# Two plain fp32 channel tiles at the start, two shift rows on TensorE, and a shorter norm in a two-layer hybrid decoder

## The chip, the cores and the metric

The kernel runs on one core of one Trainium2 chip. The metric is the device time of one execution in microseconds (us), lower is better. A core has five engines with a queue each that is worked in order: PE (TensorE, matrix products; its weight loads are listed as PEld), DVE (VectorE), ACT (ScalarE), POOL (GpSimd) and SP (SyncE, which here only issues transfers). On this kernel a difference of less than about 0.3% (3 us) cannot be told from no change.

## The reference, cut to what matters

Two layers, sequence of 256 tokens, width 1024, fp32. `rms_norm` without its gain is folded with the modulation, and `h` feeds one wide input projection and later the FFN:

```python
mod = c_act @ w_ada[l] + b_ada[l]
sh1, sc1, gt1, sh2, sc2, gt2 = jnp.split(mod, 6, axis=-1)
h = modulate(rms_norm(x, norm_mix[l]), sh1, sc1)     # h * (1 + scale) + shift
p = h @ w_in[l]
# p -> dilated attention, RWKV-7 scan, chunked spatial gating, three branch gates -> merged
x = x + gt1[:, None, :] * (merged @ w_out[l])
h = modulate(rms_norm(x, norm_ffn[l]), sh2, sc2)
x = x + gt2[:, None, :] * conv_gated_ffn(h, ...)
# after the last layer: rms_norm(x, norm_final)
```

## The kernel before

Activations lie transposed: a channel tile is 128 channels by 256 tokens, and a product over the width of 1024 adds eight of them (`k` = 0 to 7). To be near fp32 in accuracy at the speed of fp32r, every operand is split in a high part (rounded to fp32r, a CAST) and a low part (the difference, a subtraction on DVE), and one product becomes three fp32r matmuls, `mm3`: high weight by high activation, high weight by low activation, low weight by high activation. The activations' parts are `hhi` and `hlo`; the weights' are `whi` and `wlo` in steady state, with `raw` and `m` as landing buffers.

The conditioning vector is turned into rows of `mod` by `ada_col`: for each block of 128 outputs either one pass of DVE over a 128x1024 block (SCALAR_TENSOR_TENSOR with an accumulator, `w` times `crow`) or eight matmuls on PE, in fp32, with one moving column (`eng == "PE"`). `ADA_ENG` chooses; before, DVE does all.

The start is special. Before anything of layer 0 can be multiplied, `x` is loaded, its squares are summed (`rstd`: squares on ACT, sums on DVE and PE, a power on POOL, a transposing matmul that spreads the result, and a copy to `rS`), and the scale and shift of channel tile `k` must be known. `SEQ` sets the order of the 28 transfers of 512 KB in that stage: for each `k` two blocks A (scale and shift of tile k) and one or two half blocks W of the weights, so that product `k` of the first six chunks (`START` = 6, `gemm_side`, twelve weight cells of 128x128 for each `k`) can run when its A and W are there. Written out: A0 A0' W0 W1 A1 A1' W2 A2 A2' W3 W4 A3 A3' W5 and so on to W11, the accent marking the shift's block. `setup` issues all this, splits the W blocks into buffers borrowed from later stages (`dests`), and calls `norm_h`, which makes `hhi` and `hlo` of each tile.

At the other three norms the work goes through `ahead`: two chunks of the next product (`AHEAD` = 2) are multiplied with `x * A` before the norm's `rS` is known (`gemm_ahead`, 96 matmuls, operands `yrh`, `yrl`, `ygh`, `ygl`), `finish` scales the result later (tile `gate`), and `norm_h` makes the rest's operands meanwhile. In layer 1, the first of these chunks gives `zx`, whose tanh feeds the products with `lora`.

None of this is issued in the order of the code. Every operation is recorded in a `Plan` with a cost and its dependencies; `flush` runs a list scheduler a hundred times with shaken priorities, keeps the best of its own estimates and then emits each engine's queue. `P.boost` raises priorities. An operation recorded by `copy` or `ts` may be given to ACT or DVE (`either`); `act` goes to ACT alone, unless it is a Copy or Identity whose scale is a column. So any edit of costs or operations reorders all queues of the program.

Of the kernel before, what the change touches and what calls it, by code (L numbers as in the profile page):

```python
# [12 lines left out]
F32 = mybir.dt.float32  # L13
F32R = mybir.dt.float32r
# [6 lines left out]
S = 256  # L21
# [40 lines left out]
]  # L62
AHEAD = 2
START = 6
SEQ = []
for _k in range(8):
    SEQ += [("A", _k, 0), ("A", _k, 1)]
# [3 lines left out]
HOLD, SHORT, WAIT, URGENT = ("DVE",), 0.5, 0.15, 10.0  # L71
BOOST = {'ahead': 30, 'norm': 100, 'rstd': 3}
MAIN = False
ADA_ENG = [['DVE'] * 8, ['DVE'] * 8]
ADA_AT = [7, 9, 11, 11, 18, 18, 22, 22, 22, 24, 24, 30] + [39 + i * 31 // 28 for i in range(28)]
ADA = []
for _l in range(L):
# [325 lines left out]
def decoder(ctx: ExitStack, tc: tile.TileContext, xT, cst_d, vec_d, wada, stream, small, lnrow, bsrow, out):  # L403
# [10 lines left out]
    def slot(tag, shape, dt=F32):  # L414

        t = pers.tile(list(shape), dt, name=f"{tag}_{len(slots.setdefault(tag, []))}", tag=tag, bufs=1)
        n = t.tensor.name
        known.add(n)
        if slots[tag]:
            last = slots[tag][-1]  # L420
            P.born[n] = {h[1] for h in P.hist.get(last, ())} | P.born.get(last, set())
        slots[tag].append(n)
        return t
# [61 lines left out]
    def mul(o, a, b):  # L485
        tt(o, a, b, OP.mult)
# [4 lines left out]
    def sub(o, a, b):  # L491
        tt(o, a, b, OP.subtract)

    def ts(o, a, s1, s2, op0, op1=None):
        if s2 is None:
            op1 = None
        ins = [a] + [x for x in (s1, s2) if x is not None and not isinstance(x, (int, float))]

        def emit():
            if op1 is None:  # L500
                nc.vector.tensor_scalar(o, a, s1, None, op0=op0)
            else:
                nc.vector.tensor_scalar(o, a, s1, s2, op0=op0, op1=op1)  # L503

        alts = [("DVE", 0.01 + 0.06 * len(ins) + _n(a) / (960 if _psum(o, a) else 1920), emit)]
        if op0 == OP.mult and op1 in (None, OP.add) and not isinstance(s1, (int, float)) and not isinstance(s2, (int, float)):
            k = {} if s2 is None else {"bias": s2}
            alts.append(("ACT", _act(a) + 0.093 * (1 + len(k)), lambda: nc.scalar.activation(
                o, a, AF.Copy if s2 is None else AF.Identity, scale=s1, **k)))
        P.either(alts, [o], ins)  # L510
# [45 lines left out]
    raws = [raws0, raws0]  # L556
    whis = [new(pers, (128, 1024), f"whi{i}", F32R) for i in range(4)]
    wlos = [new(pers, (128, 1024), f"wlo{i}", F32R) for i in range(4)]
    bdw = [slot(f"bd{i}", (128, 2048), F32R) for i in range(3)]
    rsy = [new(pers, (128, 3, 16), f"rs{i}") for i in range(3)]  # L560
    banks = {"mm": [new(psum, (128, 512), f"bkm{i}") for i in range(3)],
             "rk": [new(psum, (128, 512), f"bkr{i}") for i in range(3)],
# [7 lines left out]
    def ring(key, lst):  # L570
        i = count.get(key, 0)
        count[key] = i + 1
        return lst[i % len(lst)]
# [78 lines left out]
    def mm3(ps, wh, wl, xh, xl, first, last):  # L652
        return [(ps, wh, xh, first, False), (ps, wh, xl, False, False), (ps, wl, xh, False, last)]
# [4 lines left out]
    def hk(k):  # L658
        return hhi[:, k, :], hlo[:, k, :]
# [41 lines left out]
    def gemm_side(m):  # L701
        pss = [bank("ff") for _ in range(min(m, 6))] + banks["at"][0:max(m - 6, 0)]
        for k in range(KT):
            for c, ps in enumerate(pss):
                g = []
                for n in range(2):
                    g += [x + (1,) for x in mm3(ps[:, n * 256:(n + 1) * 256], *cells[(k * m + c) * 2 + n], *hk(k),
                                                k == 0 and n == 0, k == KT - 1 and n == 1)]
                pe(g, MAIN)
        return pss  # L710

# [43 lines left out]
        pe([(pr[:, t * 128:(t + 1) * 128], y[:, t:t + 1].to_broadcast([128, 128]), ident) for t in range(2)])  # L755
        acopy(rS, pr[:, 0:S])

    def norm_h(l, which, tmp):
        A = amod[:, l, which * 8:which * 8 + 8]
        B = mod[:, l, which * 24:which * 24 + 8]  # L760
        for k in range(KT):
            v = ring("nv", tmp)
            mul(v, x[:, k, :], rS)
            ts(v, v, A[:, k:k + 1], B[:, k:k + 1], OP.mult, OP.add)
            acopy(hhi[:, k, :], v)
            sub(hlo[:, k, :], v, hhi[:, k, :].bitcast(F32))

# [445 lines left out]
    def setup(W):  # L1215
        P.boost = 4000.0
        turn = dma(vec, vec_d)
        for j in range(4):
            turn = dma(x[:, 2 * j:2 * j + 2, :], xT[:, 2 * j:2 * j + 2, :], seq=turn)
        tc = acol[:, 0:8]  # L1220
        act(tc, ccol, AF.Tanh, scale=0.5)
        ts(tc, tc, 1.0, 0.5, OP.add, OP.mult)
        mul(ccol, tc, ccol)
        for n in range(2):
            ps = bank("mm")
            pe([(ps[:, k * 128:(k + 1) * 128], ccol[:, 4 * n + k:4 * n + k + 1].to_broadcast([128, 128]), ident)
                for k in range(4)])
            acopy(crow[:, n * 512:(n + 1) * 512], ps)
        for l in range(L):
            ts(dv[:, l, 0:14], vv(l, "mu", 0, 14), -1.0, 1.0, OP.mult, OP.add)  # L1230
            ts(dv[:, l, 14:22], vv(l, "w0", 0, 8), 0.5, None, OP.mult)
            ts(dv[:, l, 22:26], vv(l, "ka", 0, 4), -1.0, 1.0, OP.mult, OP.add)
            ts(dv[:, l, 26:34], vv(l, "bada", 8, 8), 1.0, None, OP.add)
            ts(dv[:, l, 34:42], vv(l, "bada", 32, 8), 1.0, None, OP.add)
        rstd(W["sq"])
        bufs = raws0 + [W[f"m{i}"] for i in range(4)] + ([W[n] for n in ("VK", "PB", "BK")] if START < 7 else [W["BK"], lora])
        last = []
        for t, (a, i, n) in enumerate(SEQ):
            P.boost = 3000.0 - 10 * t
            w = ring("first", bufs)  # L1240
            d = turn = dma(w, (stream if a == "W" else wada)[i][:, n * 1024:(n + 1) * 1024], seq=turn)
            P.boost = 0.0
            if a == "A":
                last.append(d)
                ada_col(*ADA[i][n], w, ADA_ENG[n][i])
                continue
            to = dests.pop(0)
            k = 1024 // len(to)
            for m, (hi, lo) in enumerate(to):
                src = w[:, m * k:(m + 1) * k]  # L1250
                acopy(hi, src)
                sub(lo, src, hi.bitcast(F32))
                cells.extend([(hi[:, o:o + 128], lo[:, o:o + 128]) for o in range(0, k, 128)])
        pos["load"] = START
        norm_h(0, 0, halves)
        return last

    W = {}
# [24 lines left out]
    def cut(hi, lo):  # L1283
        return [(hi[:, i:i + 1024], lo[:, i:i + 1024]) for i in range(0, hi.shape[1] - 1023, 1024)]
# [1 line left out]
    short = [slot(n, (128, 512), F32R) for n in ("kkn", "tt", "s20", "s21", "sig", "aa", "cs", "gt", "zk", "zr", "zv", "zx")]  # L1286
    dests += [[(a, b)] for a, b in [(whis[0], wlos[0]), (whis[1], wlos[1])]
              + [(y[0].rearrange("p a b -> p (a b)")[:, 0:1024], y[1].rearrange("p a b -> p (a b)"))
                 for y in (yrw, ygw)] + cut(bdw[0], bdw[1]) + cut(bdw[2][:, 0:1024], bdw[2][:, 1024:2048])]
    dests += [[(short[i], short[i + 1]), (short[i + 2], short[i + 3])] for i in (0, 4, 8)]  # L1290
    count["whi"] = count["wlo"] = 2
    if START > 5:
# [2 lines left out]
    if START > 6:  # L1295
        g = [slot(f"gate{i}", (128, 512), F32R) for i in range(4)]
        dests += [[(g[0], g[1]), (g[2], g[3])], [(slot("PB", (128, 1024), F32R), slot("VK", (128, 1024), F32R))]]
    del dests[2 * START:]

    head = None  # L1300
    for l in range(L):
# [267 lines left out]
```

## Time and profile before

| what | value |
|---|---|
| median of 3 runs | 1022.81 us (1021.56 to 1024.1) |
| the profiled execution, own time | 1023.31 us |
| its span, first to last instruction | 1021.5 us |
| PE busy | 975.9 us, 96% |
| DVE busy | 906.6 us, 89% |
| ACT busy | 530.2 us, 52% |
| matmul records | 7674 |
| mean granted TensorE clock | 0.987 |
| HBM read | 212.12 MB |

A product in plain fp32 appears in the profile as two records, an fp32r one as a single record. A row of the timeline gives the start in us, the time in us, the engine, the line, the operation, output and inputs, the shape, a count, and in brackets the idle time ahead of it with what ended it. A row that merges several instructions gives the time from the first start to the last end. Times of a busy PE overlap, so the spacing of starts, not the time of one, tells its rate.

### The profile page before, as it was taken

To read this page: it belongs to the slowest core of one execution; us is meant where nothing else is said; L and a number is where in the kernel's file an instruction comes from. 1 tells how busy PE (TensorE), PEld (TensorE's weight loads), DVE (VectorE), ACT (ScalarE), POOL (GpSimd) and SP (SyncE) were. 2 spreads that over 40 slices of the span, in tenths; PEclk is the share of its full clock that TensorE was granted. 3 is DMA by queue.
4 is the path that set the end of the run, shared out by engine and by line. 5 is a ranking of instruction groups with operands and counts; after the bars stand their busy time and mean duration, and the time that the engine had idled before them with its cause. 6 is when DMAs were issued, how large, how long until landed. Compare 5 with 4: busy or idle time off the path is not lost. (4 is left out here: it accounts for less than half of the span.)

```text
span 1021.5 us, 19783 instructions
## 1 busy us (share of the span) xinstructions
PE 975.9 (96%) x7674; PEld 931.3 (91%) x7674; DVE 906.6 (89%) x1913; ACT 530.2 (52%) x909; POOL 37.4 (4%) x27
## 2 busy tenths in 40 slices
PE   2999999899999999999999999999999999999996
PEld 2988989799999999998889899998999999999886
DVE  6998999999979999999999999799867789878763
ACT  4473575675544744444447465656733555343341
POOL 0020000000000000000010110100000000000000
PEclk9999999899999999999997999999999999999998
DMA  9888575566777768789894644364435646555541
GB/s 343 345 287 266 189 234 175 174 216 206 244 261 271 231 220 300 260 285 337 320 324 132 226 151 149 124 191 146 140 119 166 213 141 221 180 184 179 188 140 42
DMA packets 70126, 217.60 MB, mean 213 GB/s; under 512 B 15120, under 2 KB 17168, under 8 KB 69520
## 3 DMA queue, kind: packets, MB, share of 16 engines
q1 hardware_dynamic: 70032, 216.34, 63.3%
q8 instruction: 60, 0.98, 0.4%
q14 instruction: 34, 0.28, 0.1%
HBM read 212.12 MB, written 4.19 MB: 212 GB/s over the span
## 5 line engine op out<-in xcount | busy, mean ns | idle before, releaser
L479 ACT CAST whi<-raw 128x1024 fp32r<-128x1024 f32 x203 | 212.0, 1048 | 229.3 <-PE bkm L455 121.5
L455 PE MATMUL bkm<-hhi,whi 128*128 128x256 f32 x1104 | 321.5, 291 | 6.8 <-ACT hhi L479 5.5
L483 DVE TENSOR_TENSOR wlo<-raw,whi 128x1024 fp32r<-128x1024 f32 (+1 forms) x293 | 292.8, 1008 | 38.8 <-ACT whi L479 37.5
L455 PE MATMUL bkm<-hlo,whi 128*128 128x256 f32 x1104 | 314.3, 285 | 5.6 <-DVE hlo L483 3.9
L455 PE MATMUL bkm<-hhi,wlo 128*128 128x256 f32 x1104 | 313.9, 284 | 0.6 <-DVE wlo L483 0.6
L455 PEld LDWEIGHTS bkm<-hhi,whi 128*128 128x128 f32 x1104 | 212.9, 193 | 13.2 <-ACT hhi L479 5.9
L455 PEld LDWEIGHTS bkm<-hlo,whi 128*128 128x128 f32 x1104 | 213.0, 193 | 7.0 <-DVE hlo L483 4.5
L455 PEld LDWEIGHTS bkm<-hhi,wlo 128*128 128x128 f32 x1104 | 212.9, 193 | 1.2 <-DVE wlo L483 1.0
L455 PE MATMUL bkr<-hhi,wlo 128*128 128x256 f32 x368 | 104.2, 283 | 0.6 <-DVE wlo L483 0.6
L455 PE MATMUL bkr<-hhi,whi 128*128 128x256 f32 x368 | 104.2, 283 | 0.0
L455 PE MATMUL bkr<-hlo,whi 128*128 128x256 f32 x368 | 104.1, 283 | 0.0
L455 PEld LDWEIGHTS bkr<-hhi,wlo 128*128 128x128 f32 x368 | 70.6, 192 | 0.8 <-DVE wlo L483 0.8
L455 PEld LDWEIGHTS bkr<-hhi,whi 128*128 128x128 f32 x368 | 70.6, 192 | 0.0
L455 PEld LDWEIGHTS bkr<-hlo,whi 128*128 128x128 f32 x368 | 70.6, 192 | 0.0
L479 ACT CAST whi<-m 128x1024 fp32r<-128x1024 f32 x39 | 40.9, 1048 | 54.0 <-PE bkr L455 19.0
L516 DVE SCALAR_TENSOR_TENSOR bd<-bd,crow 128x1024 f32<-128x1024 f32 x52 | 63.2, 1220 | 2.4 <-DMA bd<-in_wada_dram 2.1
L483 DVE TENSOR_TENSOR wlo<-m,whi 128x1024 fp32r<-128x1024 f32 x45 | 55.0, 1221 | 11.0 <-ACT whi L479 11.0
L731 POOL TENSOR_TENSOR rs<-rs,vec 128x8 f32<-128x8 f32 (+2 forms) x17 | 26.4, 1555 | 736.3 <-DVE rs L503 720.6
L516 DVE SCALAR_TENSOR_TENSOR raw<-raw,crow 128x1024 f32<-128x1024 f32 x35 | 42.7, 1219 | 3.1 <-DMA raw<-in_wada_dram 3.0
L455 PE MATMUL bkm<-ygh,whi 128*128 128x256 f32 (+1 forms) x156 | 45.0, 289 | 0.0
L455 PE MATMUL bkm<-ygl,whi 128*128 128x256 f32 x156 | 43.8, 281 | 0.3 <-DVE ygl L483 0.3
L455 PE MATMUL bkm<-ygh,wlo 128*128 128x256 f32 (+1 forms) x156 | 43.7, 280 | 0.0
(540 smaller groups left out, 2038.6 us busy)
## 6 DMA issues: line engine op xcount, KB each, us to landing
raw<-in_stream_dram SPq DMA_DIRECT2D x237, 512.0 KB, 4.7
bd<-in_wada_dram SPq DMA_DIRECT2D x52, 512.0 KB, 5.8
m<-in_stream_dram SPq DMA_DIRECT2D x48, 512.0 KB, 4.8
raw<-in_wada_dram SPq DMA_DIRECT2D x35, 512.0 KB, 5.0
m<-in_wada_dram SPq DMA_DIRECT2D x6, 512.0 KB, 10.2
scx<-x SPq DMA_DIRECT2D x2, 1024.0 KB, 9.5
x<-scx SPq DMA_DIRECT2D x2, 1024.0 KB, 5.4
x<-in_xT_dram SPq DMA_DIRECT2D x4, 256.0 KB, 4.9
```

The costliest lines, as they stand in the source:

```text
L455: nc.tensor.matmul(m[0], m[1], m[2], start=m[3], stop=m[4], skip_group_check=len(m) > 5)
L479: P.either([("ACT", _act(a), lambda: nc.scalar.copy(o, a)), ("DVE", 0.07 + _n(a) / (960 if _psum(o, a) else 1920), lambda: nc.vector.tenso ...
L483: P.add("DVE", 0.07 + _n(a) / 960, lambda: nc.vector.tensor_tensor(o, a, b, op=op), [o], [a, b])
L516: P.add("DVE", c, lambda: nc.vector.scalar_tensor_tensor(o, a, s, b, op0=op0, op1=op1, **k), [o, accum], ins)
L731: P.add("POOL", {1: 0.6, 2: 1.65, 8: 2.65}[_n(xc)], lambda: nc.gpsimd.tensor_tensor(y, xc, minus_half.to_broadcast(list(xc.shape)), op=OP. ...
```

## The change

Three edits, and the reordering that follows from them.

1. `NATIVE` = 2: for `k` = 0 and 1 the first six chunks are multiplied in plain fp32. Their three W half blocks (W0, W1, W2) land in `bd0` and `bd1`, now fp32 tiles, and are used as they are: no CAST, no subtraction. `norm_h` writes those two tiles of `h` in fp32 into `plain` (the second half of `bd1`), and `gemm_side` issues one fp32 matmul for a cell instead of three fp32r ones. `hhi` and `hlo` of these tiles are still made, for later chunks.
2. The shift rows of tiles 0 and 1 (A0', A1') are made by `ada_col` on PE: eight fp32 matmuls of one moving column instead of a DVE pass of 128x1024.
3. `norm_h` of the other tiles: before `x*rS` (DVE), times scale plus shift (DVE or ACT), CAST to `hhi` (ACT or DVE), subtraction to `hlo` (DVE). Now `x*A*rS` in one DVE instruction, one ACT instruction that adds the shift and rounds to `hhi`, and one DVE instruction `(v + shift) - hhi` to `hlo`. In the start stage the splits' CASTs are fixed to ACT.

```diff
+NATIVE = 2
-ADA_ENG = [['DVE'] * 8, ['DVE'] * 8]
+ADA_ENG = [['DVE'] * 8, ['PE', 'PE', 'DVE', 'DVE', 'DVE', 'DVE', 'DVE', 'DVE']]
...
-    bdw = [slot(f"bd{i}", (128, 2048), F32R) for i in range(3)]
+    bdw = [slot(f"bd{i}", (128, 2048), F32 if i < 2 else F32R) for i in range(3)]
...
-                    g += [x + (1,) for x in mm3(ps[:, n * 256:(n + 1) * 256], *cells[(k * m + c) * 2 + n], *hk(k),
-                                                k == 0 and n == 0, k == KT - 1 and n == 1)]
+                    wh, wl = cells[(k * m + c) * 2 + n]
+                    first, last = k == 0 and n == 0, k == KT - 1 and n == 1
+                    o = ps[:, n * 256:(n + 1) * 256]
+                    g += [(o, wh, plain[k], first, last, 1)] if wl is None else [
+                        x + (1,) for x in mm3(o, wh, wl, *hk(k), first, last)]
...
-    def norm_h(l, which, tmp):
+    def norm_h(l, which, tmp, full=0):
...
-            mul(v, x[:, k, :], rS)
-            ts(v, v, A[:, k:k + 1], B[:, k:k + 1], OP.mult, OP.add)
-            acopy(hhi[:, k, :], v)
-            sub(hlo[:, k, :], v, hhi[:, k, :].bitcast(F32))
+            v = plain[k] if k < full else v
+            stt(v, x[:, k, :], A[:, k:k + 1], rS, OP.mult, OP.mult)
+            if k < full:
+                act(v, v, AF.Identity, bias=B[:, k:k + 1])
+                acopy(hhi[:, k, :], v)
+                sub(hlo[:, k, :], v, hhi[:, k, :].bitcast(F32))
+                continue
+            act(hhi[:, k, :], v, AF.Identity, bias=B[:, k:k + 1])
+            stt(hlo[:, k, :], v, B[:, k:k + 1], hhi[:, k, :].bitcast(F32), OP.add, OP.subtract)
...
-            w = ring("first", bufs)
+            mine = a == "W" and 8 * (2 * i + n) < NATIVE * START * 2
+            w = own.pop(0) if mine else ring("first", bufs)
...
+            if mine:
+                cells.extend([(w[:, o:o + 128], None) for o in range(0, 1024, 128)])
+                continue
...
-                acopy(hi, src)
+                act(hi, src, AF.Copy)
...
-        norm_h(0, 0, halves)
+        norm_h(0, 0, halves, NATIVE)
...
+    own = [bdw[0][:, 0:1024], bdw[0][:, 1024:2048], bdw[1][:, 0:1024]]
+    plain = [bdw[1][:, 1024 + k * S:1024 + (k + 1) * S] for k in range(NATIVE)]
+    del dests[2 * START - NATIVE * START // 4:]
+    count["whi"] = count["wlo"] = 3
```

What the scheduler makes of it at the three places that matter. First PE's queue at the very start: `bka` and `bkm` are PSUM banks, `vec` holds the identity and a column of ones, `rs` the result of the power, `sq` the squares. Before:

```order
L453 MATMUL bkm1_94<-vec_66 128x128 x4
L453 MATMUL bkm0_93<-vec_66 128x128 x4
L455 MATMUL bka0_99<-vec_66,sq0_108 128x1 x4
L455 MATMUL bka0_99<-vec_66,sq1_109 128x1 x2
L453 MATMUL bka1_100<-vec_66,rs0_90 128x128 x2
L455 MATMUL bkm2_95<-hhi_75,whi0_79 128x256
L455 MATMUL bkm2_95<-hlo_76,whi0_79 128x256
L455 MATMUL bkm2_95<-hhi_75,wlo0_83 128x256
```

Now:

```order
L456 MATMUL bka0_99<-vec_66,sq1_109 128x1 x2
L456 MATMUL bka0_99<-vec_66,raw0_77 128x1 x8
L454 MATMUL bka1_100<-vec_66,rs0_90 128x128 x2
L456 MATMUL bka1_100<-vec_66,raw1_78 128x1 x8
L456 MATMUL bkm2_95<-bd1_0_88,bd0_0_87 128x256 x2
L456 MATMUL bkm1_94<-bd1_0_88,bd0_0_87 128x256 x2
L456 MATMUL bkm0_93<-bd1_0_88,bd0_0_87 128x256 x2
L456 MATMUL bkr1_97<-bd1_0_88,bd0_0_87 128x256 x2
L456 MATMUL bkm2_95<-bd1_0_88 128x256 x2
L456 MATMUL bkr2_98<-bd1_0_88,bd0_0_87 128x256 x2
```

The two shift rows (8 matmuls each, from `raw0` and `raw1`) stand one ahead of the spreading transposes of `rs` and one ahead of the first real product, which is now fp32.

Second, DVE's queue from the first block A0 on. Before:

```order
L516 SCALAR_TENSOR_TENSOR raw0_77,acol_71<-raw0_77,crow_68 128x1024
L516 SCALAR_TENSOR_TENSOR amod_74<-acol_71,dv_69,vec_66 128x1
L516 SCALAR_TENSOR_TENSOR raw0_77,acol_71<-raw0_77,crow_68 128x1024
L503 TENSOR_SCALAR rs0_90<-bka0_99 128x2
L483 TENSOR_TENSOR mod_70<-acol_71,vec_66 128x1
L480 CAST whi0_79<-raw1_78 128x1024
L483 TENSOR_TENSOR wlo0_83<-raw1_78,whi0_79 128x1024
L483 TENSOR_TENSOR wlo1_84<-raw1_78,whi1_80 128x1024
```

Now:

```order
L517 SCALAR_TENSOR_TENSOR raw0_77,acol_71<-raw0_77,crow_68 128x1024
L517 SCALAR_TENSOR_TENSOR amod_74<-acol_71,dv_69,vec_66 128x1
L504 TENSOR_SCALAR rs0_90<-bka0_99 128x2
L517 SCALAR_TENSOR_TENSOR raw1_78,acol_71<-raw1_78,crow_68 128x1024
L484 TENSOR_TENSOR mod_70<-bka0_99,vec_66 128x1
L517 SCALAR_TENSOR_TENSOR amod_74<-acol_71,dv_69,vec_66 128x1
L517 SCALAR_TENSOR_TENSOR bd1_0_88<-x_67,amod_74,rS_73 128x256 x2
L484 TENSOR_TENSOR hlo_76<-bd1_0_88,hhi_75 128x256
```

The pass over A0' and the splits of W0 and W1 are gone from here; the sum of squares (`rs`) is read right after A0, and the first two tiles of the norm follow A1.

Third, DVE's queue at the norm of layer 1, around the moment when `rS` is known. Before:

```order
L483 TENSOR_TENSOR wlo0_83<-raw0_77,whi0_79 128x1024
L516 SCALAR_TENSOR_TENSOR bd0_1_146,acol_71<-bd0_1_146,crow_68 128x1024
L520 TENSOR_REDUCE wb_72<-bkr0_96 128x1
L516 SCALAR_TENSOR_TENSOR amod_74<-acol_71,dv_69,vec_66 128x1
L483 TENSOR_TENSOR wlo1_84<-raw0_77,whi1_80 128x1024
L483 TENSOR_TENSOR gate0_0_142<-bkm2_95,rS_73 128x256
L483 TENSOR_TENSOR gate0_0_142<-bkr0_96,rS_73 128x256
```

Now:

```order
L484 TENSOR_TENSOR wlo3_86<-raw0_77,whi3_82 128x1024
L484 TENSOR_TENSOR mod_70<-acol_71,vec_66 128x1
L517 SCALAR_TENSOR_TENSOR amod_74<-acol_71,dv_69,vec_66 128x1
L484 TENSOR_TENSOR mod_70<-acol_71,vec_66 128x1 x2
L517 SCALAR_TENSOR_TENSOR amod_74<-acol_71,dv_69,vec_66 128x1
L521 TENSOR_REDUCE wb_72<-bkr0_96 128x1
L517 SCALAR_TENSOR_TENSOR amod_74<-acol_71,dv_69,vec_66 128x1
L481 COPY rS_73<-bka1_100 128x256
L484 TENSOR_TENSOR gate0_0_142<-bkm2_95,rS_73 128x256
L484 TENSOR_TENSOR gate0_0_142<-bkr0_96,rS_73 128x256
```

The copy of `rS` moves from ACT to DVE, and no 128x1024 pass stands between it and `finish` any more. In PE's queue the spreading transposes of that norm stand behind 48 matmuls of `gemm_ahead`, before behind 54.

More of the change, by code (lines that the diff above doesn't have):

```diff
@@ L1288, in decoder @@
               + [(y[0].rearrange("p a b -> p (a b)")[:, 0:1024], y[1].rearrange("p a b -> p (a b)"))
-                 for y in (yrw, ygw)] + cut(bdw[0], bdw[1]) + cut(bdw[2][:, 0:1024], bdw[2][:, 1024:2048])]
+                 for y in (yrw, ygw)] + cut(bdw[2][:, 0:1024], bdw[2][:, 1024:2048])]
     dests += [[(short[i], short[i + 1]), (short[i + 2], short[i + 3])] for i in (0, 4, 8)]
@@ L1297, in decoder @@
         dests += [[(g[0], g[1]), (g[2], g[3])], [(slot("PB", (128, 1024), F32R), slot("VK", (128, 1024), F32R))]]
-    del dests[2 * START:]
+    own = [bdw[0][:, 0:1024], bdw[0][:, 1024:2048], bdw[1][:, 0:1024]]
+    plain = [bdw[1][:, 1024 + k * S:1024 + (k + 1) * S] for k in range(NATIVE)]
+    del dests[2 * START - NATIVE * START // 4:]
+    count["whi"] = count["wlo"] = 3
     head = None
```

## The prediction

> **What bounds the kernel now.** I read the page's busy shares and its forty slices first, then the busy time by stretches.
>
> ```profile
> span 1021.5 us, 19783 instructions
> PE 975.9 (96%) x7674; PEld 931.3 (91%) x7674; DVE 906.6 (89%) x1913; ACT 530.2 (52%) x909; POOL 37.4 (4%) x27
> PE   2999999899999999999999999999999999999996
> ```
>
> ```profile
> core 0: us, PE busy (x) PEld busy (x) DVE busy (x) ACT busy (x) POOL busy (x), PEclk, DMA share, GB/s
> 25.00:60.00 35.00, 34.97 (x282) 34.77 (x282) 34.42 (x71) 17.03 (x31) 5.38 (x3) 1.00 0.91 343
> 60.00:200.00 140.00, 130.94 (x1019) 122.05 (x1019) 133.84 (x312) 86.87 (x146) 8.04 (x5) 0.98 0.66 214
> 300.00:520.00 220.00, 219.03 (x1684) 211.74 (x1684) 216.64 (x423) 107.99 (x164) 2.02 (x2) 1.00 0.81 279
> 520.00:560.00 40.00, 36.78 (x272) 35.54 (x270) 38.88 (x87) 26.47 (x47) 5.03 (x3) 0.87 0.65 208
> ```
>
> PE is busy nearly everywhere except in the first slice. In 300 to 520 it has 1 us of idle time in 220, so a shorter norm for the FFN of layer 0, which lies in there, can bring nothing. What a change can win is the time before PE starts, PE's idle time (9.1 us in 60 to 200), and the stretch around the norm of layer 1, 520 to 560, where 3.2 us are idle and the granted clock is 0.87. DVE is close behind PE (34.42 of 35 in the start's products), so whoever wants PE earlier must relieve DVE too.
>
> **The start, before.** Timeline rows of the engines, in order of time:
>
> ```profile
> 9.28 2.72 PE L455 MATMUL bka<-vec,sq 128*128 128x1 f32 x12 [2.96 <-DVE sq L483]
> 10.67 1.23 DVE L516 SCALAR_TENSOR_TENSOR raw<-raw,crow 128x1024 f32<-128x1024 f32 x1 [1.45 <-DMA raw<-in_wada_dram]
> 14.72 0.69 PE L453 MATMUL bka<-vec,rs 128*128 128x128 f32 x2 [2.72 <-POOL rs L731]
> 15.45 0.37 ACT L479 COPY rS<-bka 128x256 f32<-128x256 f32 x1
> 22.18 1.05 ACT L479 CAST ygh<-PB 128x1024 fp32r<-128x1024 f32 x1 [0.98 <-DMA PB<-in_stream_dram]
> 24.64 0.58 PE L455 MATMUL bkm<-hlo,whi 128*128 128x256 f32 x1 [3.11 <-DVE hlo L483]
> 25.23 0.41 PE L455 MATMUL bkm<-hhi,whi 128*128 128x256 f32 x1
> 25.45 0.41 PE L455 MATMUL bkm<-hlo,whi 128*128 128x256 f32 x1
> 27.30 1.05 ACT L479 CAST bd<-raw 128x1024 fp32r<-128x1024 f32 x1 [1.03 <-DMA raw<-in_stream_dram]
> 28.31 0.28 PE L455 MATMUL bkm<-hhi,whi 128*128 128x256 f32 x1
> 28.43 0.28 PE L455 MATMUL bkm<-hlo,whi 128*128 128x256 f32 x1
> 52.68 1.22 DVE L483 TENSOR_TENSOR wlo<-m,whi 128x1024 fp32r<-128x1024 f32 x1
> 61.72 1.18 PE L455 MATMUL bkr<-zx,lora 64*128 64x256 f32 x8
> ```
>
> Three instructions waited for a transfer: A0 at 10.67 (block 0 of the 28), W3 at 22.18 (block 9) and W5 at 27.30 (block 13). That is (27.30 - 10.67) / 13 = 1.28 us a block, so A1 lands at 15.8, A1' at 17.1 and the last, W11, at 45.2 at the earliest. PE's stream begins at 24.64, held by `hlo` of DVE. It runs at 0.22 us a matmul at first (25.23 to 25.45) and at 0.12 from about 28 on (28.31 to 28.43); without a gap it reaches the `lora` products at 61.72. From 28 on some 271 of the 288 matmuls take 271 x 0.12 = 32.4 us and end at 60.4; other small products take the remaining 1.3.
>
> **The start, now.** *Shift rows on PE.* Eight fp32 matmuls are 16 passes. The 12 passes of one column at 9.28 took 2.72 us, 0.22 each, so one row costs 3.5 us of PE. For A0' that lies in PE's idle time but ahead of the transposes of `rs`: it may begin when `rs` has been read, about 12.3, and ends at 15.9, after the power is done. Transposes 0.69 and copy 0.37 put `rS` at 17.0, 1.2 us later than the 15.8 of before. DVE's stall at A1 ends no earlier (15.8 + 1.2), so this delay is covered by A1; if the cover went, it would cost those 1.2. For A1' it is on the path: landing at 17.1, PE is busy until 20.6, and the first fp32 product stands behind it. The first tile of `h` needs `rS`, one DVE instruction and one of ACT, about 18.3, so PE's own row decides: start 20.6 instead of 24.64.
>
> *Plain fp32.* A full fp32 product of 256 columns:
>
> ```profile
> 129.68 1.05 PE L455 MATMUL bkr<-tt,cst 128*128 128x256 f32 x4
> 130.38 0.47 PE L455 MATMUL bkm<-hhi,whi 128*128 128x256 f32 x1
> 130.69 0.28 PE L455 MATMUL bkm<-hlo,whi 128*128 128x256 f32 x1
> ```
>
> Two such products (four records) and one fp32r matmul fill 129.68 to 130.69; less 0.12 that is 0.89, so 0.445 each, against 3 x 0.12 = 0.36. The 24 cells cost PE 2.1 us more. No row shows fp32 at the slow rate of the start. It lies between 0.445 (no slowing) and 0.89 (half); I take 0.85, since the fp32r rows at 25.23 and 28.31 show almost a halving. With 3.4 us of it, as before: 4 products by 24.0, 20 at 0.445 by 32.9, the other 216 fp32r matmuls by 58.8, small products 1.3: 60.1. Against 61.72 that is a gain of 1.6. Ends: 3.2 if fp32 is not slowed at all (24 x 0.445 from 20.6 on), 0 if the slow phase lasts twice as long (8 products in 6.8 us, 16 behind).
>
> The Trainium skill ("TensorE: Matmul & The Clock Gate", section "What's actually happening") says that the array runs at half clock until one window of about 3.4 us was busy, the window running free of the kernel. The 3.4 us from 24.64 to 28 agree. By that rule the 16 passes from 17.1 to 20.6 could count as the busy window and the fp32 products would begin at full rate; the 12 passes at 9.28 stayed slow to their end, but lasted less than a window. The result by it is the second rival.
>
> *DVE and transfers behind it.* DVE loses two passes over A blocks and three splits, 5 x 1.22 = 6.1 us (row 52.68 for one), and some CASTs go to ACT, which was half idle (17.03 of 35). The next tiles are in time: following DVE's new queue with 1.22 a 1024 pass and 0.4 a 256 one, the last tile's `hlo` comes at about 51, before 53, and its 36 matmuls would end at 56, before PE arrives there. The last W block, at 45.2 plus a CAST of 1.05 and a split of 1.22, is not late either. So PE's own work ends this stage.
>
> **The norms.** Two FFN norms lie where PE never waits: zero. The norm of layer 1's mixers is different.
>
> ```profile
> 528.39 0.38 PE L453 MATMUL bka<-vec,rs 128*128 128x128 f32 x2
> 528.88 0.37 ACT L479 COPY rS<-bka 128x256 f32<-128x256 f32 x1
> 528.89 1.22 DVE L516 SCALAR_TENSOR_TENSOR bd<-bd,crow 128x1024 f32<-128x1024 f32 x1
> 530.23 1.22 DVE L483 TENSOR_TENSOR wlo<-raw,whi 128x1024 fp32r<-128x1024 f32 x1
> 531.37 0.42 DVE L483 TENSOR_TENSOR gate<-bkm,rS 128x256 f32<-128x256 f32 x1
> 532.41 0.51 ACT L508 ACTIVATE zx<-gate,dv 128x256 f32<-128x256 f32 x1 [0.38 <-DVE gate L501]
> 533.48 0.28 PE L455 MATMUL bkr<-ygl,whi 128*128 128x256 f32 x1
> 534.08 0.48 DVE L516 SCALAR_TENSOR_TENSOR zx<-gate,vec,zx 128x255 f32<-128x255 f32 x1
> 534.87 0.41 ACT L473 ACTIVATE zx<-zx 64x256 f32<-64x256 f32 x1
> 536.12 1.53 PE L455 MATMUL bkr<-zx,lora 64*128 64x256 f32 x8 [2.37 <-ACT tt L473]
> 542.74 1.42 DVE L483 TENSOR_TENSOR hlo<-sq,hhi 128x256 fp32r<-128x256 f32 x4
> 543.55 0.58 PE L455 MATMUL bkm<-hlo,whi 128*128 128x256 f32 x1 [0.82 <-DVE hlo L483]
> 546.77 0.46 PE L455 MATMUL bkm<-hhi,whi 128*128 128x256 f32 x1
> ```
>
> Count from the transposes, T = 528.39. `rS` is there at T + 0.9, but DVE is in a pass over `bd` and a split and takes up `finish` only at T + 3.0. The chain gate, `zx`, tanh releases `lora` at T + 7.7, while PE ran out of look-ahead at T + 5.2. The last `hlo` comes at 544.2, and the second half of the next chunk starts at 546.77, T + 18.4.
>
> In the new queue the transposes stand six matmuls earlier (0.7 us), DVE waits for them, copies `rS` itself by T + 1.0, and `finish` follows at once. With 0.34 a product of two tensors, 0.40 a SCALAR_TENSOR_TENSOR of 256 (the rows of 0.42 and 0.48 overlap by that much), `zx` is done by T + 3.5 and the tanh, behind two norm instructions on ACT, by T + 4.2. The look-ahead lasts until T + 5.9 (48 matmuls), so the wait of 2.37 us goes. What is late next is `hlo`: 32 DVE instructions from the copy to the last `hlo`, 16 of them norm (6.4 us), the others `finish`, shifts and a scan (5.9): T + 13.3, and the first half chunk ends at T + 13.9. Before it was T + 18.4; with the 0.7 that is 5 us. PE is again less than half busy meanwhile and may fall to the slow rate for part of the next half chunk, as it did at 543.55 to 546; I take off 1.2: 3.8. Ends: 5.0, and 1.0, if what comes out of the chain earlier only waits for the splits that were pushed behind it.
>
> **The sum.** 1.6 + 3.8 = 5.4. The rest of the program is reordered as well; its cost I put at zero, between -3 and +3, a third of the idle time in 60 to 200 either way. Span 1021.5 - 5.4 = 1016.1; this execution took 1.8 more than its span, 1023.31, and the median of the runs is 0.5 below it: 1016.1 + 1.8 - 0.5 = 1017.4.
>
> **The rivals.**
>
> *DVE gives it back (same).* PE is only just ahead of DVE in most of 60 to 650 (216.64 of 220 in one stretch). The passes and splits pushed behind `finish` must be done soon after, and PE then waits for `wlo`. For it: DVE loses only some 6 us of work in layer 0 and next to none in layer 1. Against it: PE meets no long wait between 547 and 600. It would leave the start's 1.6 alone: 1021.2.
>
> *The warm start (faster).* If the 16 passes wake the clock, fp32 runs at 0.445 at once: 3.2 + 3.8 = 7.0: 1015.8. The 12 slow passes at 9.28 speak against it. It is the Trainium skill's window rule, of the page and section named above, applied to those passes.
>
> *The edit does not do what it says (same).* PE's first products could start late, if A1' is read late or fp32 stays slow for 7 us: start 0, and a norm gain near its low end, 1.0: 1021.8.
>
> *A new wait in layer 0's mixers (slower).* There PE already waits once for a bank that DVE has to free:
>
> ```profile
> 187.34 0.76 PE L455 MATMUL bkm<-whi,hhi 128*128 128x512 f32 x1 [3.17 <-DVE zv L516]
> ```
>
> The wait is 3.2 us and the slow matmuls behind it cost about as much again. The reordered queue could hold two such waits more: 2 x 6.4 - 5.4 = 7.4 us slower, 1030.2. It decides from a loss of 8.5 us on (5.4 and the 3.1 that are 0.3%).
>
> **How the numbers follow.** Forecast 0.52, warm start 0.08: together 0.60 below 1019.7, which is 0.3% under the median. DVE gives it back 0.23 and the failing edit 0.07: 0.30 within 0.3%. New wait 0.10: slower. The likeliest case is 1017.4. For eight in ten the range reaches down to 1012 (both upper ends, 3.2 + 5.0, give 1014.6, and 2.6 of the 3 of the reordering) and up to 1023.5, past the cases of the same side; what lies outside is the new wait and the far ends.
>
> **What would show it.** The fp32 products begin at about 20.6 right behind the second shift row, start 0.8 to 0.9 apart at first and 0.445 later. The first `lora` products come at about 60. Around the norm of layer 1, PE no longer waits between the look-ahead and `lora`, and the second half chunk starts about 14 us behind the transposes. The forecast is wrong if PE's idle time in 60 to 200 grows by more than 3 us, or if DVE's splits hold PE in 545 to 600.

## The result: 0.64% slower, and where the profile puts it

The changed kernel takes 1029.82 us, the median of 4 runs (1028.23 to 1033.3), against 1022.74 of the kernel before in the same comparison; the ratio is 1.0064, with an interval of 1.0041 to 1.0087. Forecast was 1017.4 in a range that ended at 1023.5. One execution of a kernel differs from another by some us: 32 executions of the kernel before on one chip went from 1019.26 to 1027.32. A single trace therefore shows a mechanism and its place; what it is worth is read from medians and their intervals.

The page of the changed kernel (busy times, and PE's forty slices):

```profile
span 1027.6 us, 19748 instructions
PE 987.1 (96%) x7682; PEld 939.1 (91%) x7682; DVE 903.1 (88%) x1893; ACT 522.3 (51%) x889; POOL 32.2 (3%) x27
PE   6989989999999999999999899999999999999996
```

PE is busy for 11 us more and DVE for 3.5 less: two rows and the fp32 products are added, and the first slice, 6 tenths instead of 2, holds most of the difference. The stretches, of the changed kernel, and the one of before that the prediction did not show (last line); the columns are the stretch, its length, the busy time of PE, PEld, DVE, ACT and POOL, the granted clock, the DMA share and GB/s:

```profile
25.00:60.00 35.00, 34.07 (x258) 32.90 (x256) 32.33 (x68) 14.65 (x26) 5.31 (x3) 1.00 1.02 397
60.00:200.00 140.00, 131.54 (x1009) 122.38 (x1010) 133.30 (x309) 84.96 (x144) 6.71 (x5) 0.96 0.59 192
300.00:520.00 220.00, 219.61 (x1684) 211.99 (x1683) 217.40 (x419) 106.29 (x159) 1.61 (x1) 1.00 0.81 276
520.00:560.00 40.00, 38.30 (x296) 37.58 (x295) 39.05 (x86) 25.91 (x44) 4.18 (x3) 0.91 0.68 230
560.00:680.00 120.00, 114.09 (x921) 107.63 (x920) 111.13 (x235) 68.49 (x114) 8.84 (x6) 0.99 0.51 164
```

```profile
560.00:680.00 120.00, 118.14 (x965) 112.05 (x964) 110.69 (x244) 70.03 (x116) 10.04 (x6) 1.00 0.52 168
```

300 to 520 is as full as it was. Around layer 1's norm, 520 to 560, PE is busy 1.5 us more than before, as the prediction wanted; right behind it, in 560 to 680, it is busy 4.0 us less. In 60 to 200 the busy time is 0.6 up, but at a clock of 0.96 instead of 0.98.

PE at the start of the changed kernel:

```profile
12.61 3.57 PE L456 MATMUL bka<-vec,raw 128*128 128x1 f32 x16 [0.47 <-DVE rs L504]
16.05 0.67 PE L454 MATMUL bka<-vec,rs 128*128 128x128 f32 x2
17.44 3.54 PE L456 MATMUL bka<-vec,raw 128*128 128x1 f32 x16 [0.73 <-DMA raw<-in_wada_dram]
20.85 4.54 PE L456 MATMUL bkm<-bd,bd 128*128 128x256 f32 x12
25.23 1.03 PE L456 MATMUL bkr<-bd,bd 128*128 128x256 f32 x4
60.58 1.13 PE L456 MATMUL bkr<-zx,lora 64*128 64x256 f32 x8
```

The start goes as forecast: rows of 3.5 us, fp32 products from 20.85 on (20.6 forecast), `lora` at 60.58 instead of 61.72. By the starts of the single records, the first four fp32 products stand some 0.85 apart, as forecast, and from 24.4 on they stand 0.43 apart. But 10 us after the `lora` products (the loras) PE stands still. That is the hand-over from the start to layer 0's mixer, and there the two kernels differ in what DVE does when. The first chunk of the mixer needs two tiles of weights, each loaded into a landing place (`raw`) and split (a CAST to `whi`, two half subtractions to `wlo`). Before, on SP, DVE and PE:

```profile
45.25 0.33 SPq L530 DMA_DIRECT2D raw<-in_stream_dram  x1
53.81 1.29 DVE L483 TENSOR_TENSOR wlo<-raw,whi 128x512 fp32r<-128x512 f32 x2
57.18 1.28 DVE L483 TENSOR_TENSOR wlo<-raw,whi 128x512 fp32r<-128x512 f32 x2
70.53 2.02 PE L455 MATMUL bkr<-BK,bd 128*128 128x128 f32 x16 [0.52 <-DVE BK L483]
```

Both splits were done before the `lora` products at 61.72, and PE's block on `BK` ended at 72.55. In the changed kernel (SP, DVE, and PE's wait):

```profile
47.88 0.33 SPq L531 DMA_DIRECT2D raw<-in_stream_dram  x1
55.12 0.88 DVE L502 TENSOR_SCALAR zx<-bkm,dv 128x256 f32<-128x256 f32 x2 [2.60 <-PE bkm L456]
60.84 0.68 DVE L481 CAST whi<-raw 128x1024 fp32r<-128x1024 f32 x1
61.83 1.28 DVE L484 TENSOR_TENSOR wlo<-raw,whi 128x512 fp32r<-128x512 f32 x2
65.17 1.27 DVE L484 TENSOR_TENSOR wlo<-raw,whi 128x512 fp32r<-128x512 f32 x2
71.26 0.68 DVE L484 TENSOR_TENSOR BK<-zk,sig 128x512 f32<-128x512 f32 x1
72.20 3.60 PE L456 MATMUL bkr<-BK,bd 128*128 128x128 f32 x16 [2.46 <-DVE BK L484]
```

DVE idles 2.60 us before the shift mixes (the instructions that write `zx`, `zk`, `zv` and `zr`), and then does 3.2 us of splits inside the mixer's chain that ends in `BK`, for which PE waits 2.46 us. PE's block on `BK` ends at 75.80, so a lead of 1.1 us has become a loss of 3.3. The load was issued 2.6 us later than before, at the moment its landing place came free: the start's transfers go round a ring of eleven places (`ring("first", bufs)`). With three tiles taken out of it (they go to `bd0` and `bd1`), the ring ends on `raw0` and `raw1`, the very places that the mixer loads into first; before it ended three places further, in `m01`, and `raw0` was free earlier.

Layer 1 of the changed kernel, PE's waits:

```profile
538.18 1.13 PE L456 MATMUL bkr<-zx,lora 64*128 64x256 f32 x8 [1.70 <-ACT tt L474]
573.91 0.79 PE L456 MATMUL bkm<-wlo,hhi 128*128 128x512 f32 x1 [2.41 <-DVE wlo L484]
591.20 0.38 PE L456 MATMUL bkm<-hhi,wlo 128*128 128x256 f32 x1 [1.21 <-DVE wlo L484]
```

What PE won at the norm it loses 20 to 40 us later, waiting for splits. (The kernel before waits there once, for 0.40 us at 574.82.) Set side by side, its products come level with those of the kernel before at 557 and 6.1 us later at 600; 6.0 us remain at the end.

### The profile page after: what moved, and what is told of

Same layout as the page of the kernel before. It is cut to its first block, busy times and chain, and to the rows that moved or that the text cites. A ratio compares the mean times of both kernels' runs of the same rounds, so it can differ in the third digit from the quotient of the medians.

```text
span 1027.6 us, 19748 instructions
## 1 busy us (share of the span) xinstructions
PE 987.1 (96%) x7682; PEld 939.1 (91%) x7682; DVE 903.1 (88%) x1893; ACT 522.3 (51%) x889; POOL 32.2 (3%) x27
## 5 line engine op out<-in xcount | busy, mean ns | idle before, releaser
L480 ACT CAST whi<-m 128x1024 fp32r<-128x1024 f32 x37 | 38.8, 1049 | 49.2 <-PE bkm L456 19.8
L735 POOL TENSOR_TENSOR rs<-rs,vec 128x8 f32<-128x8 f32 (+2 forms) x17 | 21.3, 1256 | 710.8 <-DVE rs L504 584.5
```

The lines of the kernel that those rows point to most:

```text
L480: P.either([("ACT", _act(a), lambda: nc.scalar.copy(o, a)), ("DVE", 0.07 + _n(a) / (960 if _psum(o, a) else 1920), lambda: nc.vector.tenso ...
L735: P.add("POOL", {1: 0.6, 2: 1.65, 8: 2.65}[_n(xc)], lambda: nc.gpsimd.tensor_tensor(y, xc, minus_half.to_broadcast(list(xc.shape)), op=OP. ...
```

## The experiments

Four theories: A, the edits gain and the new order of the mixers loses; B, the edits cost by themselves; C, the hand-over costs, by the ring's end and the splits' place; D, any new draw of the planner's order costs, since the order of before is a favourable one. (The planner is the list scheduler in `flush`; a draw is what it makes of one seed.) To hold the order while changing the code, most kernels carry a written-out list in place of the planner's rounds; the operations, their dependencies and semaphores are the program's own:

```diff
-        best, rng = None, random.Random(SEED)
...
-        for o in best[1]:
-            o.alts[o.on][2]()
+        for i in order:                  # fixed list: which operation next,
+            ops[i].on = engine[i]        # and on which of its engines
+            ops[i].alts[ops[i].on][2]()
```

**Edits and order, exchanged.** The first kernel has the edits of the changed kernel, its own order in the start and the order of before from 60 us on; the others vary this:

> All edits of the changed kernel, but from the end of the start stage on every engine issues in the order (and with the choices between ACT and DVE) of the kernel before. Theory A (the new order of the mixers costs, the edits do not): the start keeps its lead of 1 to 2 us, layer 1's norm its old order and so little more, the loss of some 11 us in 60 to 300 and 560 to 740 goes: 1019.5 to 1022 us, about 1021. Theory B (the edits cost by themselves, by ACT's and DVE's load or the fp32 products): near the changed kernel, 1027 to 1031.

> As the run with the edits in the old order, but around layer 1's norm (some 500 to 560 us) the order of the changed kernel is kept, where the loras stand later in PE's order and the half chunks sooner. Theory A: the lead of 2.9 us that the changed kernel won there comes on top of the start's: 1016.5 to 1020 us, about 1018. Theory B: 1026 to 1031.

> The kernel before with none of the edits; only in the mixers of both layers (60 to 300 and 560 to 750 us) its instructions stand in the order of the changed kernel. Theory A: it loses there what the changed kernel lost, 8 to 11 us: 1030 to 1034 us. Theory B: the order is worth nothing, 1021 to 1025.

> The changed kernel as it is, with only the mixer of layer 1 (560 to 750 us) in the order of the kernel before. Theory A: the 6 us that were lost there come back and the 4.9 of layer 0's mixer stay lost: 1022.5 to 1025 us. Theory B: 1028 to 1031.

Measured, ratio to the kernel before (1022.68 us in this comparison) with its interval:

| order and edits | us | ratio |
|---|---|---|
| edits, old order from 60 us on | 1028.86 | 1.0057 (1.0040 to 1.0075) |
| the same, new order at layer 1's norm | 1026.48 | 1.0032 (1.0016 to 1.0049) |
| no edits, new order in both mixers | 1029.32 | 1.0066 (1.0043 to 1.0088) |
| changed kernel, old order in layer 1's mixer | 1028.79 | 1.0048 (1.0026 to 1.0071) |

All four lose, so A and B both fall in their simple form: with the edits, the old order of the mixers does not help, and the new order costs as much without the edits. In all four traces the loss begins in the same place: a lead of 0.4 to 1.0 us over the kernel before at 62 us is a loss of 3.0 to 5.6 at 80. In the three with the edits the cut at 60 us had left the first chunk's splits behind the loras' result, where the changed kernel has them. That is theory C. In the kernel without the edits they stand ahead of it, as before, and its loss is the order's alone (DVE's second split, PE's loras, and PE's wait):

```profile
56.21 1.28 DVE L576 TENSOR_TENSOR wlo<-raw,whi 128x512 fp32r<-128x512 f32 x2
60.76 1.18 PE L548 MATMUL bkr<-zx,lora 64*128 64x256 f32 x8
64.33 0.50 PE L548 MATMUL bkm<-whi,hhi 128*128 128x512 f32 x1 [2.39 <-DVE zr L609]
```

**The ring, moved on.** The edit is one line, `count["first"]` being where the ring begins; eleven places, so that 3 gives the changed kernel the end that the kernel before had, and 8 gives the kernel before the end of the changed one:

```diff
     count["whi"] = count["wlo"] = 3
+    count["first"] = 3
```

> All edits, with one line more: the ring of landing places of the start begins three places further on, so that it ends on the place where it ended before the three tiles left it, and the first chunk's loads find their places free as early as before. The start's own work stands in the changed kernel's order; everything else, the first chunk's two splits on DVE ahead of the loras' result among it, in the order of the kernel before. Theory C (the hand-over from the start to layer 0's mixer costs: the shifted ring makes the first chunk's loads late and its splits, 4.5 us of DVE's work, go behind the loras' result and into the mixer's chain): the 5 to 6 us lost at 60 to 80 in every kernel with the edits so far go away, 1020 to 1023 us. Theory A's rest (any order but the one found for the kernel before is worse) and theory B (the edits cost): 1027 to 1030.

> As the run with the ring moved on, and around layer 1's norm the changed kernel's order. Theory C: the gain of 2 to 3 us that this order brought on top of the edits in the old order (1026.5 against 1028.9) comes here too: 1017 to 1021 us. The others: 1025 to 1028.

> The kernel before with none of the edits and one line more: the ring of landing places begins eight places on, so that it ends where the changed kernel's ends (on the place that the first chunk needs next); planned anew. In its order both splits of the first chunk stand behind the loras' result. Theory C: it loses most of 5 us there, 1025.5 to 1030. If the hand-over costs nothing: 1021 to 1025.

> The kernel before with another seed for the planner's draws and nothing else. In its order the first split of the first chunk is cut in two around the loras' result and the second stands behind it. Theory C: a part of the same loss, 1024 to 1029. A theory that the planner's draws do not matter on the chip: 1021.5 to 1024.5. A theory that the kernel before is a lucky draw in all stages: 1028 and more.

Measured against 1024.33 us of before: 1027.02, ratio 1.0024 (1.0006 to 1.0043); 1025.34, 1.0012 (1.0002 to 1.0022); 1028.42, 1.0049 (1.0034 to 1.0065); 1039.12, 1.0129 (1.0089 to 1.0170). The line and the splits' old place take 3.4 us off the edits in the old order (1.0057 to 1.0024), less than the 5 to 6 that the traces had suggested. The other way round the line costs 5 us, but with a new draw. What a draw alone can cost is the surprise: another seed, and nothing else, 13 us.

**The norm edit alone, and more draws.** The first two have `norm_h` as changed except in the start stage, no fp32 products and no rows on PE; the last two are `SEED = 3` in the kernel before and `SEED = 2` in the changed one.

> The kernel before with the norm edit alone (7 of 8 norms' worth: all but the one of the start stage, which stays as it was; no fp32 products, no rows on PE), everything in the order of the kernel before. If the norm edit itself neither gains nor costs in the old order: 1022 to 1024 us where the kernel before takes 1023. If its longer last step on DVE or its load on ACT costs: 1025 to 1028. If it gains by itself what the prediction saw in layer 1's norm (3.8): 1018 to 1020.

> As the run with the norm edit alone, with the changed kernel's order around layer 1's norm (500 to 556 us), where the half chunks stand ahead of the loras. By the pairs run so far (2.4 and 1.7 us gained by that order) 1.5 to 3 us faster than the norm edit in the old order, and so 1019.5 to 1022 us, ahead of the kernel before; if what the order gains is lost again in layer 1's mixer: the same as the norm edit in the old order.

> The kernel before with a third seed for the planner's draws. In its order the first chunk's splits stand ahead of the loras' result on DVE, as in the kernel before. Theory C alone (the hand-over decides): 1022 to 1026 us. Theory D (every new draw of the order costs somewhere, and the first seed was a favourable one): 1027 to 1040.

> The changed kernel with the second seed. Theory D: anywhere from 1023 to 1040 us, some us away from the changed kernel's 1030. If the edits set the time and the draw does not: 1028 to 1032.

Against 1023.71 us of before: norm edit in the old order 1023.08, ratio 0.9991 (0.9972 to 1.0009); with the new order at layer 1's norm 1022.52, 0.9989 (0.9970 to 1.0008); third seed 1027.17, 1.0024 (1.0004 to 1.0044); changed kernel with the second seed 1031.49, 1.0062 (1.0040 to 1.0083). So the norm edit shows neither a cost nor a gain. The order at layer 1's norm was worth some 2.5 and 1.2 us in the two pairs before and 0.2 here; the intervals of each pair overlap. The trace of this last kernel shows why it isn't more, in stretches and in PE's waits:

```profile
520.00:560.00 40.00, 37.31 (x280) 35.05 (x280) 39.41 (x86) 26.22 (x44) 2.33 (x2) 1.00 0.69 226
560.00:590.00 30.00, 26.75 (x202) 24.54 (x201) 28.98 (x69) 15.75 (x27) 2.59 (x2) 0.94 0.58 201
```

```profile
562.99 0.50 PE L547 MATMUL bkm<-wlo,hhi 128*128 128x512 f32 x1 [1.12 <-DVE wlo L575]
575.74 0.39 PE L547 MATMUL bkm<-hhi,wlo 128*128 128x256 f32 x1 [1.10 <-DVE wlo L575]
577.52 1.97 PE L547 MATMUL bka<-m,m 128*64 128x128 f32 x16 [1.04 <-DVE m L575]
```

DVE is busy 39.41 of 40 us and 28.98 of 30. Set against the kernel before, the same products of PE come some 5.5 us earlier at 522, 9.8 at 557 and 5.1 at 586: the 4 us won are gone after three waits for DVE. The draws give D its weight: three seeds of the kernel before lie at 1, 1.0024 and 1.0129, and the first of them is the one in use.

**The place of the splits, by itself.** In the first kernel only the two splits move, in the second only DVE's part of them; every other row of DVE, ACT and PE around it stands as it stood (on SP, in the second, two loads that use the freed places again move back too). The third and fourth divide the start edit, each on top of the norm edit in the old order.

> The changed kernel in its own order, but for one thing: the first chunk's two splits (two casts, on ACT, and four half subtractions on DVE) stand ahead of the shift mixes, in the 2.6 us in which DVE and the 4.7 us in which ACT waits there, instead of behind the loras' result. Theory C (the hand-over): 3 to 5 us less than the changed kernel, 1024.5 to 1027 us. If the place of the splits is worth nothing: 1028.5 to 1031.

> The kernel before in its own order, but for one thing: DVE's part of the first chunk's two splits (1.28 + 0.68 + 1.28 us) stands behind the loras' result instead of ahead. Theory C: PE's first products of that chunk and the mixer's chain wait for it, 2.5 to 5 us more, 1025.5 to 1028.5 us. If it is worth nothing: 1022.5 to 1024.5.

> The norm edit in the old order, and the two shift rows on PE; no fp32 products. If the rows are free, as the prediction had it (they run where PE has nothing else): 0 to 1 us from the norm edit alone (1023). If they hold up the first mean or the first products: 1024.5 to 1027.

> The norm edit in the old order with the fp32 products and the ring moved on, and the two shift rows back on DVE. If the remaining cost of the start edits (3.4 us between 1.0024 and 0.9991) is the fp32 products': 1025 to 1027.5. If it is the rows': 1022 to 1024.5.

Against 1024.06 us of before: 1031.69, 1.0069 (1.0050 to 1.0088); 1028.00, 1.0036 (1.0015 to 1.0056); 1027.23, 1.0033 (1.0019 to 1.0047); 1025.41, 1.0011 (0.9999 to 1.0022).

The kernel before loses 3.7 us when its splits go behind the loras' result; PE's first product of the chunk then waits for `zr`, which stands behind them on DVE:

```profile
66.25 0.76 PE L548 MATMUL bkm<-whi,hhi 128*128 128x512 f32 x1 [4.07 <-DVE zr L609]
```

But the changed kernel wins nothing when its splits go ahead. Its rows on ACT say why:

```profile
54.15 1.05 ACT L571 CAST whi<-raw 128x1024 fp32r<-128x1024 f32 x1 [3.05 <-DMA raw<-in_stream_dram]
56.95 1.05 ACT L571 CAST whi<-raw 128x1024 fp32r<-128x1024 f32 x1 [1.75 <-DMA raw<-in_stream_dram]
```

The tiles are not there. Ahead of the mixes the splits hold up the mixes, behind them they hold up the chain. My expectation that only their place counted was wrong: the loads are late, and that leaves no good place.

**The ring in a fixed order, both ways.** The kernel before in its own order with `count["first"] = 8`, and the changed kernel in its own order with `count["first"] = 3`, its two loads as early in SP's queue as before and its splits ahead of the mixes:

> The kernel before in its own order throughout, with the ring of landing places begun eight places on and so ending as the changed kernel's does. If the late loads cost: the two splits stand ahead of the mixes and wait for them, as in the changed kernel with its splits ahead, 3 to 5 us more than before, 1026 to 1029 us. If the ring costs nothing: 1022.5 to 1025.

> The changed kernel with the ring moved on by three places, so that it ends as in the kernel before, the first chunk's two loads as early in SP's queue as there, and its two splits ahead of the mixes; all else in the changed kernel's order. If the late loads cost it 4 to 5 us: 1024 to 1026.5 us. If not: 1029 to 1031.

Against 1022.80 us: 1032.16, ratio 1.0087 (1.0065 to 1.0108), and 1025.79, 1.0030 (1.0014 to 1.0047). One line costs the kernel before 9 us. It changes which buffer is whose and no instruction; the queues of PE, DVE and ACT stay as they were, and on SP `lora` and one block A change places with the loads next to them. The rows of SP, DVE and PE in that kernel:

```profile
51.15 0.68 SPq L623 DMA_DIRECT2D raw<-in_stream_dram  x1
60.66 0.69 DVE L573 CAST whi<-raw 128x1024 fp32r<-128x1024 f32 x1 [2.95 <-DMA raw<-in_stream_dram]
67.98 1.23 DVE L609 SCALAR_TENSOR_TENSOR raw<-raw,crow 128x1024 f32<-128x1024 f32 x1 [4.13 <-DMA raw<-in_wada_dram]
69.67 2.08 PE L548 MATMUL bkr<-zx,lora 64*128 64x256 f32 x8 [5.84 <-DVE zv L609]
```

The second load goes out at 51.15 (before: 47.63) and lands at 60.66 behind others, and the mixes queued behind its CAST on DVE are late by that. Then the pass over a block A waits another 4.13 us for its transfer, which is late too. The last part of `zv` stands behind that pass, and the loras wait for it: they come at 69.67 instead of 61.72. And the changed kernel with the ring moved back, SP and ACT:

```profile
43.51 0.33 SPq L622 DMA_DIRECT2D raw<-in_stream_dram  x1
50.62 1.05 ACT L571 CAST whi<-raw 128x1024 fp32r<-128x1024 f32 x1
52.24 1.05 ACT L571 CAST whi<-raw 128x1024 fp32r<-128x1024 f32 x1 [0.57 <-DMA raw<-in_stream_dram]
```

Issued 4.4 us earlier, the tiles are split before the mixes begin (at 56.5), and half of the changed kernel's loss (3.5 us, 1.0064 to 1.0030) is gone. The same place of the splits without the ring moved had won nothing (1.0069), so the earlier loads bring it.

No version beats the kernel before measurably. The norm edit with the new order at layer 1's norm is the lowest, at 0.9989 (0.9970 to 1.0008).

## Why the prediction was wrong, point by point

- **The start stage**: what it described happened, at 20.85 and 60.58 for the forecast 20.6 and 60.1; its lead was 1.1 us by that row, not 1.6. The 0.85 taken for a slow fp32 product was right, though no row showed it. The failure is at its end. "The next tiles are in time" followed the start's own tiles and stopped at the last W block. It did not ask which places the start's transfers leave behind and who loads into them next. That step, the transfers behind the change, is the one that failed first, at a cost of some 3.5 of the changed kernel's 6.5 us, with the reordered splits that follow from it.
- **The rows on PE**: the first was called covered by A1's stall, the second was counted in the start at 20.6. Four kernels, each with the norm edit in the old order, divide them from the fp32 products: 0.9991 without either, 1.0033 with the rows, 1.0011 with the fp32 products, 1.0024 with both (these two with the ring moved on, and the start in a new order). Without fp32 products the rows cost 4.3 us, some 2.4 either way. With them, as in the changed kernel, they make 1.3 us, some 2.2 either way, which shows no cost. The fp32 products make 0.6 on the mean of their two pairs, no difference. PE's rows, with the norm edit alone (the first two) and with the rows added:

```profile
14.57 0.69 PE L545 MATMUL bka<-vec,rs 128*128 128x128 f32 x2 [2.41 <-POOL rs L823]
24.50 0.58 PE L547 MATMUL bkm<-hlo,whi 128*128 128x256 f32 x1 [3.12 <-DVE hlo L575]
15.63 0.67 PE L545 MATMUL bka<-vec,rs 128*128 128x128 f32 x2
25.93 0.58 PE L547 MATMUL bkm<-hlo,whi 128*128 128x256 f32 x1 [3.11 <-DVE hlo L575]
```

  The first row delays the spreading of `rs` from 14.57 to 15.63 and the first products from 24.50 to 25.93; at the loras 1.0 us of it is left (62.20 and 63.22). Where the rest of the 4.3 us comes from was not found. And with the fp32 products but without the rows these products begin 2.6 us sooner, at 18.24 instead of 20.85, of which 1.1 is left at the loras (59.96, against 61.03 with the rows and all else equal):

```profile
18.24 5.19 PE L547 MATMUL bkm<-bd,bd 128*128 128x256 f32 x12 [3.53 <-ACT bd L565]
23.27 1.89 PE L547 MATMUL bkr<-bd,bd 128*128 128x256 f32 x8
```

- **The FFN norms**: zero, as forecast (219.61 of 220).
- **Layer 1's norm** was priced at 3.8 us. Of the 2.37 us wait ahead of `lora` 1.70 stayed, but PE's gain in 520 to 560 is there. It did not reach the end: the low end of that term, 1.0, "if what comes out of the chain earlier only waits for the splits", was the case: the pairs put the order's part at 0.2 to 2.5 us, and the norm edit with that order gains 1.1 over the kernel before (0.9989), in an interval of 3.1 gained to 0.8 lost. In the changed kernel's trace the 2.9 us won at this norm were followed by 6.3 lost. The rival "DVE gives it back" described it rightly; its argument against ("no long wait between 547 and 600") read the old order, in which DVE had not been pushed. One of the prediction's own signs of failure, splits holding PE in 545 to 600, is the row at 573.91. The other, PE's idle time in 60 to 200 growing by more than 3 us, did not come: it went from 9.1 to 8.5, while the clock in that stretch fell from 0.98 to 0.96.
- **The reordering at zero, between -3 and +3**: this term and its bound were mis-sized. It came from a third of PE's idle time in one stretch. Measured, a new draw of the order costs the kernel before 2.5 us with the third seed and 13 with the second, and the changed kernel with the second seed is at 1.0062. The new order in the mixers without any edit costs 6.7 us, with the splits in their old place. The parts do not add up: this order alone costs 6.7, the edits in the old order cost 5.8, and both together, in the changed kernel, 6.5. Why is open.
- **The rivals**: the warm start did not happen. The window rule of the Trainium skill ("TensorE: Matmul & The Clock Gate", section "What's actually happening") would have let the second row, 17.44 to 20.98, count as a busy window; the first four products behind it still ran 0.85 apart, and at 0.43 only from 24.4 on, so the trace gives no sign that single-column passes count. "A new wait in layer 0's mixers" had the right sign and, at 1030.2, nearly the right time, but by another mechanism: not a PSUM bank, but a landing place and the order of the mixers. That the time agrees is luck.

What is settled: the place on which the ring ends costs, both ways, through the loads that wait for it; the splits' late place costs the kernel before 3.7 us; the new order of the mixers costs 6.7 without any edit; the rows cost where no fp32 products follow them; the norm edit and the fp32 products show no cost. What stays open is the rest of the changed kernel's loss after the ring, 1.0030. The trace of that last kernel (an execution 2.3 us above its median) puts it in layer 1's mixer, not in the start. At the norm's spreading transposes it is level with the kernel before (528.07 against 528.39), at the next norm's it is 4.6 us behind (831.78 against 827.17). PE waits there for a split as in the changed kernel:

```profile
571.95 0.50 PE L547 MATMUL bkm<-wlo,hhi 128*128 128x512 f32 x1 [2.61 <-DVE wlo L575]
```

From the one norm's transposes to the other's, the twelve kernels with the old order of layer 1's mixer took 298.7 to 301.3 us in their traces. The four with the changed kernel's order took 301.9 to 303.7, the one without edits among them: some 2.5 us more on the mean. So that order is the likelier cause of the rest. Giving the changed kernel the old order there brought it to 1.0048 from 1.0064, inside the intervals. No run took the rows out of the changed kernel, and none moved alone its ring of `whi` and `wlo`, which begins three places on (the last line of the diff).

## What to carry to other kernels

When an edit takes buffers out of a ring or puts some in, ask where the ring ends and who loads into that place next: one line that shifted a ring by eight places and changed no instruction cost 9 us. Behind a scheduler that draws, the order in use may be the best of several draws (here the best of three), so an edit that triggers a new one can start some us behind; hold the order fixed to learn what the edit itself is worth. Here a chain shortened in a stretch where another engine is 97% busy gave back what it had won within some 35 us.

## What the runs showed of the hardware

Two kernels with the same queues up to 497 us, the edits with the ring moved on, ran the same products at a different clock. The spacing of 512-column products in the first (64.45 to 64.75 and on) and the second (66.42 to 66.85):

```profile
64.45 0.47 PE L547 MATMUL bkm<-whi,hlo 128*128 128x512 f32 x1
64.75 0.40 PE L547 MATMUL bkm<-whi,hhi 128*128 128x512 f32 x1
64.99 0.39 PE L547 MATMUL bkm<-wlo,hhi 128*128 128x512 f32 x1
```

```profile
66.42 0.63 PE L547 MATMUL bkm<-wlo,hhi 128*128 128x512 f32 x1
66.85 0.63 PE L547 MATMUL bkm<-whi,hlo 128*128 128x512 f32 x1
```

In the first they stand 0.24 apart after 1.3 us of slow ones, in the second still 0.43 apart. The granted clock was 0.50 up to 64.6 and 1.00 behind it in the first, and 0.50 up to 69.4 in the second. The wait before these products was 0.46 us in one and 0.79 in the other. The first of them stand 1.1 us apart in the two traces (63.46 and 64.58), and a later product 5.6 (186.73 and 192.37), though the queues are the same; how much of that the clock makes is not shown. Whoever takes one trace's lead at a point for the worth of an edit reads that chance too. The same section of the Trainium skill says that the window runs free of the kernel and that the number of slow matmuls varies from run to run; the rows agree with the varying number and do not show the window.

The slow phase of the start differed too: 3.4 us before, 3.5 in the changed kernel (20.85 to 24.4), and about 4.8 in the kernel with fp32 products and no rows (0.84 a product from 18.24 on, 0.43 from 23.05).
